# Gate and up products of two feed-forward blocks by a Strassen form: seven block products for eight, tokens in two halves

## The chip, the cores and the metric

The kernel runs on one core of a Trainium2 chip. The metric is the device time of one execution in microseconds (us); the runs shown of the kernel before have a median of 1450.88 us (three runs, 1450.59 to 1451.72).

## What is computed

A decoder trunk of two layers over 512 tokens of width 1024, in float32. Layer 0 mixes tokens with two kinds of attention, layer 1 with a Mamba-2 block; after each mixer stands a SwiGLU feed-forward block with a hidden width of 2816, on a normalized input. Cut to what matters here:

```python
def rmsnorm(x, w, eps=NORM_EPS):
    y = xf * lax.rsqrt(jnp.mean(xf * xf, axis=-1, keepdims=True) + eps)
    return (y * w.astype(jnp.float32)).astype(x.dtype)

def swiglu(h, w_gate, w_up, w_down):
    return (jax.nn.silu(h @ w_gate) * (h @ w_up)) @ w_down

h = h + swiglu(rmsnorm(h, ffn_norm[layer]), ffn_w_gate[layer], ffn_w_up[layer], ffn_w_down[layer])
```

## The kernel before, in words

**Layout.** Activations are held transposed: 8 chunks of 128 features (partitions) by 512 tokens. A weight tile of 128 input features by 128 output features is the stationary operand of a matmul, 512 tokens are the moving one, and the result is 128 output features by 512 tokens in one PSUM bank.

**Two-part operands.** For precision each operand is split in two float32r parts, high and low: ScalarE casts the tile to its high part, VectorE subtracts that from the tile to get the low part. A product is three matmuls, high by high, high by low, low by high (`proj`, L340 to L342). The inputs of a feed-forward block are `xh`, `xl`; the weights are `whi`, `wlo`.

**The weight stream.** `Stream` (L83) walks a list of weight loads of 128 x 1024 floats, 512 KB each: SyncE loads them into `wraw` (3 buffers, L104), ScalarE casts to `whi` (L117) and VectorE subtracts to `wlo` (L118), 3 buffers of each. `next` (L124) has the split of the load two places ahead issued before the matmuls of the present one. One load serves two chunks of one group of four output tiles, 24 matmuls.

**The feed-forward block** (`ffn`, L745). Gate and up come in 11 groups `t` of four output tiles (two of gate, then two of up). Each group has four loads, 8 chunks k, and 96 matmuls into four PSUM banks of the pool `acc`, which has four. Its evacuation `evac_gu` makes silu of a gate tile (ScalarE, L763), multiplies it by the up tile (VectorE, L767) and splits the product to `hh`, `hl` (L771, L772) for the down projection. The reciprocal root of the norm, `rbc`, is only known some time after the block starts: groups 0 and 1 run on inputs that have the norm's weight alone, and their results are multiplied by `rbc` when they are evacuated (L759). During group 1 the chunks are normalized and split anew, one by one (`normalized`, L354), and groups 2 to 10 read those. The down projection then takes 22 hidden tiles through `proj` (L340 to L342 again, tile `hh`); in layer 1 its last output tile is done by `finish` in two halves of 256 tokens (L1145 to L1147).

**What sets the order.** Work that lies beside the matmuls is a generator in `bg`; `proj` calls `bg.step(steps)` after each chunk k. The instructions are traced in program order. A planner then writes each engine's queue ahead of the run: among the instructions whose inputs it reckons ready when the engine comes free, the one that was traced first goes next. The engine takes its queue in that fixed order.

Of the kernel before, what the change touches and what calls it, by code (L numbers as in the profile page):

```python
# [25 lines left out]
LAMBDA_INIT = 0.8 - 0.6 * math.exp(-0.3 * 0)  # L26
KK = 2
LOOK = 2


SSD_ORDER = [
# [51 lines left out]
class Stream:  # L83


    def __init__(self, nc, pool, plan):
        self.nc, self.pool, self.plan = nc, pool, plan
        self.loaded = 0
        self.split = 0
        self.raw = {}  # L90
        self.parts = {}
        self.pos = 0
# [2 lines left out]
    def cuts(i, w):  # L95
        return ((0, w // 2), (w // 2, w)) if i == 0 else ((0, w),)

    def load_to(self, n):
        while self.loaded < min(n, len(self.plan)):
            ap, w = self.plan[self.loaded]  # L100
            i = self.loaded
            raw = self.pool.tile([P, 1024], F32, tag="wraw", name=f"wraw{i}", bufs=3)
# [3 lines left out]
            self.loaded += 1  # L106

    def split_to(self, n):
        while self.split < min(n, len(self.plan)):
            i = self.split  # L110
            self.load_to(i + 1)
            _, w = self.plan[i]
            raw = self.raw.pop(i)
            hi = self.pool.tile([P, 1024], F32R, tag="whi", name=f"whi{i}", bufs=LOOK + 1)
            lo = self.pool.tile([P, 1024], F32R, tag="wlo", name=f"wlo{i}", bufs=LOOK + 1)
            for c0, c1 in self.cuts(i, w):
                self.nc.scalar.copy(hi[:, c0:c1], raw[:, c0:c1])  # L117
                self.nc.vector.tensor_tensor(out=lo[:, c0:c1], in0=raw[:, c0:c1], in1=hi[:, c0:c1].bitcast(F32),  # L118
                                             op=ALU.subtract)
            self.parts[i] = (hi, lo)  # L120
            self.split += 1
            self.load_to(i + 3)

    def next(self):  # L124
        self.split_to(self.pos + LOOK + 1)
        r = self.parts.pop(self.pos)
        self.pos += 1
        return r


class Work:
# [21 lines left out]
def build(nc, tc, a):  # L153
    ctx = ExitStack()
    with ctx:
# [10 lines left out]
        def uid(s):  # L166
            count[0] += 1
            return f"{s}_{count[0]}"
# [16 lines left out]
        for t in range(2):  # L185
            plan += [(a["w_aout"][t * 4 + p], 1024) for p in range(4)]

        def ffn_plan(l):
            r = []
            for t in range(11):  # L190
                r += [(a[f"w_gu{l}"][t * 4 + p], 1024) for p in range(4)]
            for t, n in enumerate(DOWN_TILES[l]):
                r += [(a[f"w_down{l}_{t}"][i], KK * n * P) for i in range(11)]
            return r

        plan += ffn_plan(0)
# [33 lines left out]
        for n, (c0, c1) in enumerate(((0, 1), (1, 3), (3, 5), (5, 8))):  # L230
            nc.sync.dma_start(htile[0][:, c0:c1, :], xv[:, c0:c1, :])
            if n < 3:
                ws.load_to(n + 1)
# [82 lines left out]
        def proj(nk, ncols, get_x, evac, token_major=False, kk=KK, steps=0, width=2, wait=0):  # L316

            nt = 4 if token_major else (ncols + P - 1) // P
            ps = [None] * nt
            for p in range(nk // kk):  # L320
                whi, wlo = ws.next()
                for q in range(kk):
                    k = p * kk + q
# [26 lines left out]
        def x0get(k):  # L350
            done_k[0] = k
            return xh[k], xl[k]

        def normalized(norm):  # L354

# [389 lines left out]
        def ffn(l, norm, nxt, after, finish=None):  # L745
            with ExitStack() as fctx:
                fp = fctx.enter_context(tc.tile_pool(name=uid("ffn"), bufs=1))
                bg.add(norm.stats())
                hid = []

                gate = {}

                def evac_gu(t, j, ps):

                    if t < 2:
                        if t == 0:
                            bg.drain()
                        v = fp.tile([P, S], F32, tag="sg", name=uid("sg"), bufs=4)
                        tt(out=v, in0=ps, in1=norm.rbc, op=ALU.mult)  # L759
                        ps = v  # L760
                    if j < 2:
                        sg = fp.tile([P, S], F32, tag="sg", name=uid("sg"), bufs=4)
                        act(sg, ps, AF.Silu)  # L763
                        gate[j] = sg
                    else:
                        sg = gate.pop(j - 2)
                        tt(out=sg, in0=sg, in1=ps, op=ALU.mult)  # L767
                        n = len(hid)
                        hh = fp.tile([P, S], F32R, tag=f"hh{n}", name=uid("hh"))
                        hl = fp.tile([P, S], F32R, tag=f"hl{n}", name=uid("hl"))  # L770
                        nc.scalar.copy(hh, sg)  # L771
                        tt(out=hl, in0=sg, in1=hh.bitcast(F32), op=ALU.subtract)  # L772
                        hid.append((hh, hl))

                for t in range(11):
# [4 lines left out]
                    if t == 1:  # L780
                        for _ in xn:
                            pass
                        bg.drain()

                c0 = 0
                for n in DOWN_TILES[l]:
                    def evac_down(j, ps, c0=c0):
                        c = c0 + j
                        tt(out=h[c], in0=h[c], in1=ps, op=ALU.add)  # L789
                        nxt.chunk(c)  # L790
                        after(c)
                    proj(22, n * P, lambda k: hid[k], evac_down)
                    c0 += n
                if finish:
                    finish(hid)
# [365 lines left out]
def pack(w, groups, korder, kk):  # L1161

    r = []
    for cols in groups:
        m = np.concatenate([w[:, c0:c0 + n] for c0, n in cols], axis=1)
        for i in range(0, len(korder), kk):
            r.append(np.concatenate([m[k * P:(k + 1) * P] for k in korder[i:i + kk]], axis=1))
    return np.ascontiguousarray(np.stack(r))


def host_layout(x, attn_norm, attn_w_in, diff_lq1, diff_lk1, diff_lq2, diff_lk2, diff_subln, attn_w_out,
# [8 lines left out]
    d["w_aout"] = pack(attn_w_out[0], half, AO_K, KK)  # L1180
    for l in range(2):
        gu = np.concatenate([ffn_w_gate[l], ffn_w_up[l]], axis=1)
        d[f"w_gu{l}"] = pack(gu, [[(t * 256, 256), (DFF + t * 256, 256)] for t in range(11)], k8, KK)
# [54 lines left out]
```

## Time and profile before

| | |
|---|---|
| median of 3 runs | 1450.88 us |
| profiled execution, its own time | 1449.53 us |
| its span, first to last instruction | 1447.7 us |
| TensorE matmuls | 6755, busy 98% of the span |
| VectorE, ScalarE | busy 55% and 47% of the span |
| mean granted TensorE clock | 0.997 |

PE is TensorE's matmuls, PEld its weight loads, DVE VectorE, ACT ScalarE, POOL GpSimd, SP SyncE. A matmul's row shows its duration in the pipeline; the pace is the distance between two starts. The same holds for DVE and ACT, whose rows can overlap a little with the next.

### The profile page before, as it was taken

The numbers are of one execution on the slowest core, as the hardware profiler recorded it, in microseconds if no ns is written. First come the engines' busy times: TensorE is split into PE (matmuls) and PEld (weight loads), VectorE is DVE, ScalarE is ACT, GpSimd is POOL, SyncE is SP. The second block draws the span as 40 slices with busy tenths as digits, with TensorE's granted clock in tenths as the row PEclk, the third lists the DMA queues.
The fourth block names the chain that finished last, engine by engine and source line by source line (L and its number), as shares of the span: only waits on it lengthen the run. The fifth ranks groups of instructions, "written<-read, shape, count | busy, mean of one in ns | idle before, by whom it ended". The sixth has DMA issues, their size and how long they took to land.

```text
span 1447.7 us, 17120 instructions
## 1 busy us (share of the span) xinstructions
PE 1421.1 (98%) x6755; PEld 1168.3 (81%) x6755; DVE 797.7 (55%) x1145; ACT 681.8 (47%) x1137; POOL 21.5 (1%) x23
## 2 busy tenths in 40 slices
PE   9999899999999999999999999999999999999997
PEld 6777678888888888877888888887888888888886
DVE  7677995572333323247787684886556333333233
ACT  6555774342232222236879767594444233232131
POOL 0000001000000000000000000000000000000000
PEclk9999999999999999999999999999999999999998
DMA  6213241223233232333323223223232333333231
GB/s 217 88 35 97 65 126 59 88 87 116 89 102 98 92 102 88 128 111 105 129 101 102 102 88 119 100 73 130 88 102 87 102 91 99 103 89 100 84 106 59
DMA packets 41712, 142.83 MB, mean 99 GB/s; under 512 B 4736, under 2 KB 6912, under 8 KB 40224
## 3 DMA queue, kind: packets, MB, share of 16 engines
q1 hardware_dynamic: 40512, 140.68, 30.6%
q8 instruction: 53, 0.87, 0.2%
q10 hardware_dynamic: 1088, 1.05, 0.2%
q14 instruction: 27, 0.22, 0.0%
q0 software_dynamic: 32, 0.00, 0.0%
HBM read 135.36 MB, written 4.26 MB: 96 GB/s over the span
## 4 chain that ended last, share of the span: by engine, by line
PE 89%; DVE 5%; ACT 3%; issue 1%; POOL 1%; DMA 0%; SPq 0%; POOLq 0%; DVEq 0%; ACTq 0%
PE acc L340 24%; PE acc L342 24%; PE acc L341 24%; PE acc L333 2%; PE acc L335 2%; PE acc L334 2%; PE misc L1003 2%; DVE e L528 2%; PE misc L978 1%; PE misc L1008 1%; DVE wlo L118 1%; PE misc L496 1%; PE misc L948 1%; DVE e L530 0%; PE misc L1030 0%
## 5 line engine op out<-in xcount | busy, mean ns | idle before, releaser
L118 DVE TENSOR_TENSOR wlo<-wraw,whi 128x1024 fp32r<-128x1024 f32 (+3 forms) x230 | 276.2, 1202 | 446.9 <-ACT whi L117 444.8
L117 ACT CAST whi<-wraw 128x1024 fp32r<-128x1024 f32 (+3 forms) x230 | 238.0, 1035 | 486.7 <-PE acc L341 415.8
L340 PE MATMUL acc<-xnh,whi 128*128 128x512 f32 x808 | 319.7, 396 | 0.0
L341 PE MATMUL acc<-xnl,whi 128*128 128x512 f32 x808 | 316.9, 392 | 0.0
L342 PE MATMUL acc<-xnh,wlo 128*128 128x512 f32 x808 | 314.5, 390 | 0.0
L342 PEld LDWEIGHTS acc<-xnh,wlo 128*128 128x128 f32 x808 | 151.7, 188 | 31.9
L340 PEld LDWEIGHTS acc<-xnh,whi 128*128 128x128 f32 x808 | 151.7, 188 | 31.3 <-DVE sg L759 0.3
L341 PEld LDWEIGHTS acc<-xnl,whi 128*128 128x128 f32 x808 | 151.8, 188 | 30.1
L340 PE MATMUL acc<-hh,whi 128*128 128x512 f32 x330 | 128.5, 389 | 0.0
L342 PE MATMUL acc<-hh,wlo 128*128 128x512 f32 x330 | 128.4, 389 | 0.0
L341 PE MATMUL acc<-hl,whi 128*128 128x512 f32 x330 | 128.4, 389 | 0.0
L340 PE MATMUL acc<-xh,whi 128*128 128x512 f32 (+1 forms) x288 | 114.4, 397 | 1.9 <-DVE vl L467 1.1
L342 PE MATMUL acc<-xh,wlo 128*128 128x512 f32 (+1 forms) x288 | 113.2, 394 | 1.2 <-DVE wlo L118 1.2
L341 PE MATMUL acc<-xl,whi 128*128 128x512 f32 (+1 forms) x288 | 113.4, 394 | 0.2 <-DVE xl L279 0.2
L341 PEld LDWEIGHTS acc<-hl,whi 128*128 128x128 f32 x330 | 61.9, 188 | 12.9
L340 PEld LDWEIGHTS acc<-hh,whi 128*128 128x128 f32 x330 | 61.9, 188 | 12.9 <-DVE h L789 0.2
L342 PEld LDWEIGHTS acc<-hh,wlo 128*128 128x128 f32 x330 | 61.9, 188 | 12.9
L340 PEld LDWEIGHTS acc<-xh,whi 128*128 128x128 f32 (+1 forms) x288 | 53.5, 186 | 14.7 <-DVE vl L467 1.3
L342 PEld LDWEIGHTS acc<-xh,wlo 128*128 128x128 f32 (+1 forms) x288 | 53.5, 186 | 13.7 <-DVE wlo L118 2.1
L341 PEld LDWEIGHTS acc<-xl,whi 128*128 128x128 f32 (+1 forms) x288 | 53.6, 186 | 11.5 <-DVE xl L279 0.6
L767 DVE TENSOR_TENSOR sg<-sg,acc 128x512 f32<-128x512 f32 x36 | 24.5, 688 | 49.7 <-PE acc L342 41.2
L340 PE MATMUL acc<-ysh,whi 128*128 128x512 f32 x128 | 50.6, 395 | 0.0
(269 smaller groups left out, 2141.5 us busy)
## 6 DMA issues: line engine op xcount, KB each, us to landing
wraw<-w_gu SPq DMA_DIRECT2D x88, 512.0 KB, 3.6
wraw<-w_down SPq DMA_DIRECT2D x33, 512.0 KB, 3.6
wraw<-w_st SPq DMA_DIRECT2D x28, 512.0 KB, 3.5
wraw<-w_ain SPq DMA_DIRECT2D x23, 512.0 KB, 3.7
wraw<-w_sz SPq DMA_DIRECT2D x16, 512.0 KB, 3.2
h<-acd SPq DMA_DIRECT2D x8, 1024.0 KB, 4.8
wraw<-w_sout SPq DMA_DIRECT2D x16, 512.0 KB, 3.3
wraw<-w_down SPq DMA_DIRECT2D x11, 384.0 KB, 3.1
```

The lines of the kernel that those rows point to most:

```text
L117: self.nc.scalar.copy(hi[:, c0:c1], raw[:, c0:c1])
L118: self.nc.vector.tensor_tensor(out=lo[:, c0:c1], in0=raw[:, c0:c1], in1=hi[:, c0:c1].bitcast(F32), op=ALU.subtract)
L333: mm(o, ah[:, bs], whi[:, wc], start=first, stop=False)
L334: mm(o, ah[:, bs], wlo[:, wc], start=False, stop=False)
L335: mm(o, al[:, bs], whi[:, wc], start=False, stop=last)
L340: mm(o, whi[:, c0:c0 + m], ah, start=first, stop=False)
L341: mm(o, whi[:, c0:c0 + m], al, start=False, stop=False)
L342: mm(o, wlo[:, c0:c0 + m], ah, start=False, stop=last)
L496: nc.tensor.transpose(ps[:, n * P:(n + 1) * P], src[:, SEG[i] + j * P:SEG[i] + (j + 1) * P], ident)
L528: nc.vector.tensor_tensor_scan(out=keep[:, ::-1], data0=keep[:, ::-1], data1=endc[:, ::-1], initial=1.0, op0=ALU.mult, op1=ALU.max)
L767: tt(out=sg, in0=sg, in1=ps, op=ALU.mult)
L1003: mm(py[:, r * 64:(r + 1) * 64], bc[:, r, cs], xdt[:, c, r * 64:(r + 1) * 64], start=True, stop=True)
```

## The change

Groups 0 and 1 of gate and up stay as they are (`CONV = 2`). The other 18 output tiles of gate and their 18 of up are done in pairs: tile i of gate and tile i of up, tokens in halves, the eight input chunks in even (first) and odd (second) ones. The product of the 2 x 2 block weights with the 2 x 2 block inputs is made of seven block products instead of eight, named 11, 12, s2, s1, s3, 22 and s4. A block product is 4 chunks x 3 matmuls of 256 tokens. It needs sums of weight blocks and of input blocks:

- The input sums (`combos`) are made once per feed-forward block while groups 0 and 1 run, with `steps=2`; they replace `normalized`. In a first part each of four chunk pairs has two normalized products, four half-width differences and the splits for 11, s2 and 22. In a second part, as the old `xh`, `xl` chunks come free, the splits for 12, s4, s1 and s3.
- The weight sums: for s1 and s3 the DMA adds while it writes (a SyncE load, then a GpSimd-issued DMA with `accum_op=add`); for s2 and s4 VectorE adds two blocks before the split.
- Loads are per pair one of 512 KB (`w_g`, kept in `wraw` until s4 is split) and five of 256 KB, two of these accumulating. The loads run one step earlier than before in the rest of the kernel too.
- After the blocks, ScalarE and VectorE copy and add partial results between two PSUM banks (`o1`, `o3`) and SBUF. Hidden tiles of the pairs are kept unsplit and are split in the down projection (`hget`), up to three ahead. The last two blocks of the last pair run after the first load of the down projection.

The diff, cut to its core:

```diff
+CONV = 2
+NPAIR = NFF - 2 * CONV
 class Stream:
...
             hi = self.pool.tile([P, 1024], F32R, tag="whi", name=f"whi{i}", bufs=LOOK + 1)
...
+            if isinstance(ap, list):
+                work = [(slice(n * 512, n * 512 + 512), b[0].block(b[1], b[2]), b) for n, b in enumerate(ap)]
...
+            for cs, src, b in work:
+                src = src() if b else src
+                self.nc.scalar.copy(hi[:, cs], src)
+                self.nc.vector.tensor_tensor(out=lo[:, cs], in0=src, in1=hi[:, cs].bitcast(F32), op=ALU.subtract)
+                if b and b[0].done(b[1], b[2]):
+                    self.load()
...
-            self.load_to(i + 3)
+            if not isinstance(ap, list):
+                self.load()
+class Pairs:
...
+        for i in range(n + 1):
+            r += [(i, "11"), (i, "12")] if i < n else []
+            if i == n:
+                break
+            r += [(i - 1, "22"), (i - 1, "s4")] if i else []
+            r += [(i, "s2"), (i, "s1"), (i, "s3")]
+        self.order = r
+    def load(self, i, raw):
+        self.first[i] = raw
+        self.nc.sync.dma_start(raw, self.w11[i])
+        if i < 2:
+            for what in ("s1", "s3", "22"):
+                self.load_side(i, what)
+    def load_side(self, i, what):
...
+        if what == "s1":
+            self.nc.sync.dma_start(t, w21)
+            self.nc.gpsimd.dma_start(t, w22, accum_op=ALU.add)
+        elif what == "s3":
+            self.nc.sync.dma_start(t, self.w11[i, :, 0:512])
+            self.nc.gpsimd.dma_start(t, w21, accum_op=ALU.add)
+        else:
+            self.nc.sync.dma_start(t, w22)
+    def block(self, i, what):
...
+            if what == "s2":
+                self.nc.vector.tensor_tensor(out=a, in0=self.side[i, "s1"], in1=a, op=ALU.add)
+            elif what == "s4":
+                self.nc.vector.tensor_tensor(out=b, in0=a, in1=b, op=ALU.add)
...
+    def done(self, i, what):
+        if what in ("s1", "s3", "22"):
+            del self.side[i, what]
+            self.load_side(i + 2, what)
+        elif what == "s4":
+            del self.first[i]
+            return True
+        return False
+        def combos(norm, fp, xs):
...
+            def split(dst, src, cs=slice(0, S)):
+                hi, lo = dst
+                nc.scalar.copy(hi[:, cs], src)
+                tt(out=lo[:, cs], in0=src, in1=hi[:, cs].bitcast(F32), op=ALU.subtract)
...
+            for c in range(NCH // 2):
...
+                for o, n in ((xa, 2 * c), (xb, 2 * c + 1)):
+                    stt(out=o, in0=h[n], scalar=vcol(norm.w, n), in1=norm.rbc, op0=ALU.mult, op1=ALU.mult)
+                yield
+                tt(out=ta[:, H[0]], in0=xa[:, H[0]], in1=xa[:, H[1]], op=ALU.subtract)
+                tt(out=ta[:, H[1]], in0=xb[:, H[1]], in1=xa[:, H[1]], op=ALU.subtract)
+                stt(out=tb[:, H[0]], in0=ta[:, H[0]], scalar=-1.0, in1=xb[:, H[1]], op0=ALU.mult, op1=ALU.subtract)
+                stt(out=tb[:, H[1]], in0=tb[:, H[0]], scalar=-1.0, in1=xb[:, H[0]], op0=ALU.mult, op1=ALU.subtract)
+                yield
...
+                split(half[0], xa[:, H[0]], H[c % 2])
...
+                split(e, tb)
...
+                yield
+            for c in range(NCH // 2):
+                while done_k[0] < 2 * c + 1:
+                    yield
...
+                e = xpair(2 * c, "xc")
+                split(e, xb)
...
+                e = xpair(2 * c + 1, "xc")
+                split(e, ta)
...
+                yield
-                for t in range(11):
-                    if t == 1:
-                        xn = normalized(norm)
-                        bg.add(xn)
-                    proj(8, 512, x0get if t == 1 else xget, lambda j, ps: evac_gu(t, j, ps), steps=1 if t < 2 else 0)
...
+                for t in range(CONV):
+                    proj(8, 512, x0get if t == CONV - 1 else xget, lambda j, ps: evac_gu(t, j, ps), steps=2)
...
+                def block(i, what, whi, wlo):
+                    if what == "11":
+                        o1[i] = bank("misc")
+                    elif what == "12":
+                        o2[i] = bank("acc")
+                    elif what == "s1":
+                        o3[i] = bank("misc")
+                    o = {"12": o2, "s1": o3, "s4": o3}.get(what, o1)[i][:, A]
...
+                    for c in range(NCH // 2):
+                        wc = slice(c * P, (c + 1) * P)
+                        ah, al = xs[what, c]
+                        mm(o, whi[:, wc], ah, start=new and c == 0, stop=False, skip_group_check=True)
+                        mm(o, whi[:, wc], al, start=False, stop=False, skip_group_check=True)
+                        mm(o, wlo[:, wc], ah, start=False, stop=end and c == NCH // 2 - 1, skip_group_check=True)
...
+                    if what == "11":
+                        sg[i] = fp.tile([P, S], F32, tag="gate", name=uid("sg"), bufs=2)
+                        nc.scalar.copy(sg[i][:, A], o1[i][:, A])
+                    elif what == "12":
+                        tt(out=sg[i][:, A], in0=sg[i][:, A], in1=o2[i][:, A], op=ALU.add)
+                    elif what == "s2":
+                        nc.scalar.copy(sg[i][:, B], o1[i][:, A])
+                    elif what == "s3":
...
+                        nc.scalar.copy(hl[:, B], o1[i][:, A])
+                        tt(out=hl[:, B], in0=hl[:, B], in1=o3[i][:, A], op=ALU.add)
+                    elif what == "s4":
...
+                        tt(out=sg[i][:, B], in0=sg[i][:, B], in1=o3[i][:, A], op=ALU.add)
+                        act(sg[i], sg[i], AF.Silu)
+                        stt(out=hl[:, A], in0=o1[i][:, A], scalar=-1.0, in1=sg[i][:, A], op0=ALU.mult, op1=ALU.mult)
+                        stt(out=hl[:, B], in0=hl[:, B], scalar=-1.0, in1=sg[i][:, B], op0=ALU.mult, op1=ALU.mult)
...
+                blocks(pr.order)
...
+                def hget(k):
+                    for n in range(k, min(k + 3, len(hid))):
+                        split_hid(n)
+                    return hid[k]
```

## Rows read from the trace of the kernel before

**Rows 1.** Page, part 1: busy time, share of the span, instructions.
```profile
PE 1421.1 (98%) x6755; PEld 1168.3 (81%) x6755; DVE 797.7 (55%) x1145; ACT 681.8 (47%) x1137; POOL 21.5 (1%) x23
```

**Rows 2.** Chain that ended last: share of the span by engine.
```profile
PE 89%; DVE 5%; ACT 3%; issue 1%; POOL 1%; DMA 0%; SPq 0%; POOLq 0%; DVEq 0%; ACTq 0%
```

**Rows 3.** Windows: stretch; PE, PEld, DVE, ACT, POOL busy; clock; DMA share; GB/s.
```profile
336.50:553.00 216.50, 216.50 (x957) 179.27 (x956) 71.85 (x76) 61.52 (x76) 0.00 (x0) 1.00 0.32 98
1310.00:1425.00 115.00, 115.00 (x529) 96.06 (x528) 37.77 (x44) 33.47 (x45) 0.00 (x0) 1.00 0.27 83
1439.50:1440.00 0.50, 0.00 (x0) 0.00 (x0) 0.00 (x0) 0.00 (x0) 0.50 (x1) 0.76 0.00 0
1440.00:1440.50 0.50, 0.38 (x2) 0.38 (x3) 0.00 (x0) 0.00 (x0) 0.06 (x1) 0.50 0.00 0
```

**Rows 4.** Timeline of PE in block zero's gate and up, 18 starts apart.
```profile
399.70 0.39 PE L340 MATMUL acc<-xnh,whi 128*128 128x512 f32 x1
...
403.78 0.39 PE L340 MATMUL acc<-xnh,whi 128*128 128x512 f32 x1
```

**Rows 5.** Timeline of PE, last projection, 22 starts apart; then its weight loads.
```profile
1434.01 0.28 PE L1146 MATMUL acc<-hl,wlh 128*128 128x256 f32 x1
...
1436.65 0.28 PE L1147 MATMUL acc<-hh,wll 128*128 128x256 f32 x1
...
L1145 PEld LDWEIGHTS acc<-hh,wlh x44: 188/192/192, 1419.8 to 1436.3; 128*128 128x128 f32 x44
```

**Rows 6.** Timeline of DVE: instructions that follow at once on each other.
```profile
824.78 0.68 DVE L993 TENSOR_TENSOR h<-h,cb 128x512 f32<-128x512 f32 x1
825.38 0.74 DVE L908 SCALAR_TENSOR_TENSOR fb<-u,vec,fb 128x510 f32<-128x510 f32 x1
...
834.61 1.22 DVE L970 TENSOR_TENSOR xdt<-xs,dtt 128x1024 f32<-128x1024 f32 x1
835.74 1.22 DVE L118 TENSOR_TENSOR wlo<-wraw,whi 128x1024 fp32r<-128x1024 f32 x1
...
837.21 0.42 DVE L991 TENSOR_TENSOR xs<-xs,vec 128x256 f32<-128x256 f32 x1
837.55 0.41 DVE L986 TENSOR_TENSOR prev<-prev,misc 128x256 f32<-128x256 f32 x1
```

**Rows 7.** Groups by line and form, DVE and ACT: busy, mean ns.
```profile
L772 DVE TENSOR_TENSOR hl<-sg,hh 128x512 fp32r<-128x512 f32 x44 | 28.4, 685 | 0.6 <-ACT hh L771 0.6
L771 ACT CAST hh<-sg 128x512 fp32r<-128x512 f32 x44 | 25.4, 618 | 2.6 <-DVE sg L767 2.6
L763 ACT ACTIVATE sg<-sg 128x512 f32<-128x512 f32 x8 | 5.0, 631 | 8.2 <-DVE sg L759 8.1
```

**Rows 8.** Timeline near the end: DVE hands over to ACT.
```profile
1428.17 0.42 DVE L1115 TENSOR_TENSOR h<-h,acc 128x256 f32<-128x256 f32 x1 [4.64 <-PE acc L1147]
...
1428.62 0.42 ACT L1116 ACTIVATE up<-h 128x256 f32<-128x256 f32 x1 [5.06 <-DVE h L1115]
```

**Rows 9.** Timeline of DVE at the start of block zero's feed-forward.
```profile
271.31 2.05 DVE L739 TENSOR_TENSOR h<-h,acc 128x512 f32<-128x512 f32 x3 [1.32 <-PE acc L342]
273.27 0.75 DVE L279 SCALAR_TENSOR_TENSOR xl<-h,vec,xh 128x512 fp32r<-128x512 f32 x1
...
277.07 0.68 DVE L739 TENSOR_TENSOR h<-h,acc 128x512 f32<-128x512 f32 x1
...
284.60 1.41 DVE L361 SCALAR_TENSOR_TENSOR xn<-h,vec,rbc 128x512 f32<-128x512 f32 x2 [2.96 <-ACT rbc L314]
...
295.15 2.80 DVE L759 TENSOR_TENSOR sg<-acc,rbc 128x512 f32<-128x512 f32 x4 [1.32 <-PE acc L342]
```

**Rows 10.** Timeline of PE: warm-up matmuls at the start.
```profile
2.29 4.01 PE L239 MATMUL misc<-warm 128*128 128x512 bf16 x9 [2.29 <-ACT warm L236]
```

**Rows 11.** Queues and DMA issues: packets, MB, share; KB, us to landing.
```profile
q1 hardware_dynamic: 40512, 140.68, 30.6%
vec<-vec POOLq DMA_DIRECT2D x1, 4.0 KB, 3.1
```

More of the change, by code (lines that the diff above doesn't have):

```diff
@@ L87, in __init__ @@
         self.nc, self.pool, self.plan = nc, pool, plan
+        self.loads = []
+        for i, (ap, w) in enumerate(plan):
+            if isinstance(ap, list):
+                self.loads += [(b[0], b[1]) for b in ap if b[2] == "11"]
+            else:
+                self.loads.append((None, i))
         self.loaded = 0
@@ L96, in cuts, with load @@
         return ((0, w // 2), (w // 2, w)) if i == 0 else ((0, w),)
[L98 to L102, printed above, removed]
+    def load(self, n=1):
+        for _ in range(n):
+            if self.loaded == len(self.loads):
+                return
+            owner, i = self.loads[self.loaded]
+            raw = self.pool.tile([P, 1024], F32, tag="wraw", name=f"wraw{self.loaded}", bufs=3)
+            self.loaded += 1
+            if owner:
+                owner.load(i, raw)
+                continue
+            ap, w = self.plan[i]
             for c0, c1 in self.cuts(i, w):
@@ L128, in next, with __init__, items, last @@
         return r
+class Pairs:
+    def __init__(self, nc, w11, w2, n):
+        self.nc, self.w11, self.w2, self.n = nc, w11, w2, n
+        self.tile = None
+        self.first = {}
+        self.side = {}
+        r = []
+        for i in range(n + 1):
[5 more added lines that the diff above has]
+        self.order = r
+    def items(self):
+        b = [(self, i, what) for i, what in self.order]
+        return [(b[i:i + 2], 1024) for i in range(0, len(b), 2)]
+    def last(self):
+        return [([(self, self.n - 1, "22"), (self, self.n - 1, "s4")], 1024)]
+    def load(self, i, raw):
[5 more added lines that the diff above has]
+    def load_side(self, i, what):
+        if i >= self.n:
+            return
+        t = self.side[i, what] = self.tile({"s1": 0, "s3": 2, "22": 4}[what] + i % 2)
+        w21, w22 = self.w2[i, 0], self.w2[i, 1]
+        if what == "s1":
[4 more added lines that the diff above has]
+            self.nc.gpsimd.dma_start(t, w21, accum_op=ALU.add)
+        else:
+            self.nc.sync.dma_start(t, w22)
+    def block(self, i, what):
+        def get():
+            first = self.first[i]
+            a, b = first[:, 0:512], first[:, 512:1024]
+            if what == "s2":
+                self.nc.vector.tensor_tensor(out=a, in0=self.side[i, "s1"], in1=a, op=ALU.add)
+            elif what == "s4":
+                self.nc.vector.tensor_tensor(out=b, in0=a, in1=b, op=ALU.add)
+            return {"11": a, "s2": a, "12": b, "s4": b}.get(what) if what not in ("s1", "s3", "22") \
+                else self.side[i, what]
+        return get
+    def done(self, i, what):
[6 more added lines that the diff above has]
+        return False
 class Work:
@@ L314, in stats, with proj @@
                 nc.scalar.copy(self.rbc, pb)
-        def proj(nk, ncols, get_x, evac, token_major=False, kk=KK, steps=0, width=2, wait=0):
+        def proj(nk, ncols, get_x, evac, token_major=False, kk=KK, steps=0, width=2, wait=0, hook=None):
             nt = 4 if token_major else (ncols + P - 1) // P
@@ L747, in ffn, with after_stats @@
                 fp = fctx.enter_context(tc.tile_pool(name=uid("ffn"), bufs=1))
+                pr = pairs[l]
+                pr.tile = lambda n: fp.tile([P, S], F32, tag=f"hh{4 + n}", name=uid("ws"))
+                done_k[0] = -1
+                xs = {}
                 bg.add(norm.stats())
+                def after_stats():
+                    while norm.rbc is None:
+                        yield
+                    yield from combos(norm, fp, xs)
+                xc = after_stats()
+                bg.add(xc)
@@ L773, in evac_gu @@
[L773 to L783 removed]
+                        tt(out=v, in0=gate.pop(j - 2), in1=v, op=ALU.mult)
@@ new lines, in blocks, with tail @@
+                def blocks(order):
+                    for m in range(0, len(order), 2):
+                        whi, wlo = ws.next()
+                        for q, (i, what) in enumerate(order[m:m + 2]):
+                            cs = slice(q * 512, q * 512 + 512)
+                            block(i, what, whi[:, cs], wlo[:, cs])
+                blocks(pr.order)
+                def tail(p):
+                    if p == 1:
+                        blocks([(NPAIR - 1, "22"), (NPAIR - 1, "s4")])
```

97 lines of the change are left out of this document (70 added, 27 removed).

## Prediction, made before the changed kernel ran

> **What bounds the kernel now.** I read the page first: TensorE's matmuls are busy 98% of the span, VectorE (DVE) 55%, ScalarE (ACT) 47% [rows 1]; but a share says little where stages differ, so I went on to the chain that ended last, 89% of which is PE [rows 2]. Then the windows of the stretch that the change touches: in block zero's feed-forward PE has no idle time, DVE works 71.85 of 216.5 us, ACT 61.52, and the DMA engines are a third busy [rows 3]. So the pace of the matmuls sets the time. The timeline of PE gives that pace: 4.08 us for 18 starts, 0.2267 us for one matmul of 512 columns [rows 4]. The same kernel already has matmuls of 256 columns with a weight load each, in its last projection: 2.64 us for 22 starts, 0.120 us each, though one weight load lasts 0.19 us [rows 5]: the loads lie under the matmuls. Half the columns cost a little more than half the time.
>
> **The matmuls.** A pair of output tiles now takes 2 x 8 x 3 = 48 matmuls of 512 columns, 48 x 0.2267 = 10.88 us. The seven blocks take 7 x 4 x 3 = 84 of 256 columns, 84 x 0.120 = 10.08 us. So 0.80 us of the 1.36 us that an eighth would be is kept; 36 pairs in two blocks give **-28.8 us**. That is the whole gain.
>
> **What the other engines must do in 10.08 us.** Of DVE I need the distance from one instruction to the next where none waits: 0.60 us for 512 elements, 0.34 for 256, 1.13 for 1024, each 0.08 shorter than its duration [rows 6]. Per pair DVE has seven subtractions for the low parts (7 x 0.605 = 4.24), two additions for s2 and s4, and evacuations of 256 columns: an addition each for 12, s3 and s4, and two products. In three places it cannot run on, unless other work is ready: behind the s2 and the s4 addition stands a cast by ACT (0.618) and behind the s4 evacuation a silu (0.631) [rows 7], each with two hand-overs of 0.03 [rows 8]. So an addition with its cast takes 0.685 + 0.618 + 0.06 = 1.36, twice 2.73; the evacuations 2 x 0.335, then 0.42 + 0.631 + 0.06 = 1.11, then 2 x 0.335: 2.45. Sum 9.41 us, under PE's 10.08. With full durations in place of distances it is 7 x 0.685 + 2.73 + 2 x 0.42 + 1.11 + 2 x 0.42 = 10.31, 0.23 over, which is 36 x 0.23 = 8 us. The bounds are 0 and +8 us; the busy stretch of rows 6 runs at distances, so I stay near the lower end: **+3 us**. ACT has seven casts, three copies and a silu, under 7 x 0.62 + 3 x 0.42 + 0.63 = 6.2 us: hidden.
>
> One wait is tight on PE: s3 accumulates in the bank that ACT must first have copied after s2, and only s1 (12 x 0.12 = 1.44 us) lies between. A cast just begun and the copy take about 0.62 + 0.42 = 1.04: it fits, so nothing; if ACT hangs behind DVE, PE waits there (rival two).
>
> **Transfers.** A pair moves 512 + 5 x 256 KB, 1.84 MB, against 1 MB. The present queue carries 140.68 MB in 30.6% of 1447.7 us, 318 GB/s at full share [rows 11]. The plain part, 1.31 MB, needs 4.1 us of 10.08. No row shows an accumulating DMA. As a plain copy its 0.26 MB would take 0.8 us of all engines; the one GpSimd-issued DMA here needs 3.1 us from issue to landing, 4 KB only [rows 11]; if two such stood in series with the rest, 4.1 + 6.2 = 10.3 us would just pass the pair's time. They are asked for two pairs (20 us) ahead, so latency is hidden and only throughput counts; I take 0, as nearer to the copy. The Trainium skill's page "DMA: Bandwidth & Descriptors" (Anatomy of one DMA) prices a GpSimd-issued DMA at about 2.0 us plus its bytes at 436 GB/s, by estimate 2.6 us for 256 KB and nothing on the sum; it says nothing of accumulation. SyncE issues two loads more per pair, GpSimd two; both queues hold little else in this stage, and each waits for buffers freed two pairs before their next use: nothing.
>
> **The seam between groups 0 and 1.** Here I expect the gain to be given back. The planner's order shows in DVE's queue: the fourth addition to `h` goes at 277.07, behind work on the earlier chunks though its matmuls had long ended [rows 9]. What was traced first goes first, once ready. Now `steps=2` traces all twelve steps of the first part of `combos` before the evacuation of group 0. They need `rbc`, first used at 284.60 [rows 9]; until then they can't start. Per chunk pair: two products of 0.66 (1.41 for two with overlap [rows 9]), four half-width operations of 0.335, a half split of 0.335 and one of 0.605: 1.32 + 1.34 + 0.34 + 0.61 = 3.6, four times 14.4. Two weight splits of 1.13 stand between: 16.7. So DVE is at this until 284.6 + 16.7 = 301.3. The last split waits for its cast, so the first evacuation slips in at 300.7 and ends at 301.4. Before, it began at 295.15, and four took 2.80 us, at PE's pace [rows 9]; so PE is done with group 0 at about 297.2. Group 1 needs the four `acc` banks that group 0 holds, and no weights of later work are split yet. PE stands 301.4 + 0.1 - 297.2 = 4.3 us. The bounds are 0, if the evacuation goes first, and 7, if all four evacuations (2.8 us) must end first. I take 4.3, which is what the banks ask for. At the end of the trace the granted clock fell from 1.00 to 0.50 (2.4 to 1.2 GHz) between 1439.5 and 1440.0 [rows 3]; PE had done little since the last projection ended at 1436.65 [rows 5]. So I expect it to fall in this pause too. At the start nine warm-up matmuls of 512 columns took 4.01 us [rows 10], 0.446 each against 0.2267: coming back costs 9 x 0.22 = 2.0 us (bounds 0 and 2; I take 2). Together 6.3 per block, twice **+12.6 us**.
>
> **The seam before the pairs.** When group 1 ends, DVE owes eight operations of evacuation, two late splits and one item's two: 12 x 0.605 = 7.3 us, of which 1.9 lie before that end. PE can go on with 11, 12, s2 and s1, 4 x 1.44 = 5.8 us: even. If 12 has to wait for its last chunk, after 1.44 + 1.08, it costs 5.4 - 2.5 = 2.9. I take 0.5, twice **+1 us**.
>
> **Costed at nothing.** The down projection now splits 18 hidden tiles per block itself: a cast and 0.605 us of DVE per 12 x 0.2267 = 2.72 us of PE; there DVE works 37.77 of 115 us [rows 3]. Without that cover it would be 18 x 1.3 per block. Loads one step earlier: PE waits for none of them.
>
> **The sum**, against the profiled execution's own 1449.5: 1449.5 - 28.8 + 3 + 12.6 + 1 = 1437.3. That execution is 1.4 us below the median, 1450.9; on the runs' scale **1439 us**.
>
> **Rivals.**
> *One: the seam is no wait.* The planner places the evacuations first, or finds other matmuls. For it: in nearly the whole trace it keeps PE busy [rows 1]; against it: rows 9. Then only the 28.8 counts: 1422, with some waits 1425. Chance 0.21.
> *Two, the other side: DVE and ACT set the pair's pace.* If ACT reaches each of its two late casts only behind an operation of 256 columns (0.42 [rows 8]), DVE's chain at full durations is 10.31 + 0.84 = 11.15 us. PE then stands before s3, and the price is (11.15 - 10.08) x 36 = 38 us, 35 more than the 3 taken: 1474. It decides at 10.08 + (28.8 - 13.6) / 36 = 10.5 us per pair: above that the change loses. For it: 9.41 of 10.08 is little slack; against: a planner can fill two of the three waits. Chance 0.20.
> *Three: the accumulating DMAs are slow.* At 4 us of all engines each, five times a copy, a pair takes 4.1 + 8 = 12.1 us: +2.0 x 36 = 73 us, 1509. For it: nothing shown. Chance 0.10.
> *Four: weight loads don't hide.* In series a block's matmul would take 0.12 + 0.19 = 0.31, the pair 26 us, 36 x 15.9 = +570: 2010. Rows 5 speak against it: starts 0.120 apart. The Trainium skill's "TensorE: Matmul & The Clock Gate" (The mechanism) has a load overlap a running matmul only when its row group differs; by that rule this rival would hold, and the trace disagrees. Chance 0.01.
>
> **How the numbers follow.** My forecast has 0.48; its own range is 1430 to 1450 (seams at their bounds, 0 to 8 us in the pairs). About 0.2% is what a measurement here can tell from no change: 1448.0 to 1453.8. Faster: 0.41 of the forecast and all of rival one, 0.62. Same: 0.07 of the forecast and 0.05 of rival two, 0.12. Slower: the rest of two, three, four: 0.26. The range takes in rival one and the lower part of rival two, up to 10.8 us per pair: 1422 to 1463.
>
> **What would show it.** Right: 256-column starts 0.120 us apart in both blocks; a pause of some 4 us before group 1 with DVE on `combos`, released by the L759 evacuation, and 0.50 clock after it. Wrong: no such pause (rival one); PE waiting for ACT's copy in each pair (two); ACT or DVE waiting for the side tiles' DMA, DMA share near 1 (three); starts over 0.2 us apart (four).

## The result: 1436.1 us, 1.0% faster

The changed kernel takes 1436.1 us (median of four, 1434.9 to 1437.3); the kernel before, beside it on the same chip, 1450.7. The ratio is 0.990, 95% interval 0.988 to 0.992. The prediction said 1439, 1422 to 1463. The profiled execution took 1434.85 us with a span of 1432.7, against 1449.53 and 1447.7 before: 15.0 us of span went.

### The profile page after: what moved, and what is told of

Its sections match the earlier page's. It is cut to its first block, busy times and chain, and to the rows that moved or that the text cites. A ratio compares the mean times of both kernels' runs of the same rounds, so it can differ in the third digit from the quotient of the medians.

```text
span 1432.7 us, 20958 instructions
## 1 busy us (share of the span) xinstructions
PE 1396.3 (97%) x8051; PEld 1208.7 (84%) x8051; DVE 974.9 (68%) x1589; ACT 789.5 (55%) x1441; POOL 83.6 (6%) x95
## 3 DMA queue, kind: packets, MB, share of 16 engines
q1 hardware_dynamic: 50880, 150.13, 31.2%
q0 software_dynamic: 10400, 18.88, 8.4%
## 4 chain that ended last, share of the span: by engine, by line
PE 85%; DVE 9%; ACT 3%; issue 2%; DMA 1%; POOL 1%; SPq 0%; DVEq 0%; POOLq 0%; ACTq 0%
PE acc L439 15%; PE acc L440 14%; PE acc L441 14%; PE misc L965 7%; PE misc L966 7%; PE misc L967 7%; PE acc L432 2%; PE acc L434 2%; PE acc L433 2%; PE misc L1224 2%; DVE e L679 2%; PE acc L967 1%; PE acc L965 1%; PE acc L966 1%; DVE wlo L136 1%
## 5 line engine op out<-in xcount | busy, mean ns | idle before, releaser
L136 DVE TENSOR_TENSOR wlo<-wraw,whi 128x512 fp32r<-128x512 f32 (+3 forms) x302 | 284.6, 952 | 264.5 <-ACT whi L135 262.5
L135 ACT CAST whi<-wraw 128x512 fp32r<-128x512 f32 (+3 forms) x302 | 248.2, 833 | 331.9 <-PE acc L440 228.0
L965 PE MATMUL misc<-xe,whi 128*128 128x256 f32 x432 | 122.4, 283 | 0.0
L966 PE MATMUL misc<-xcl,whi 128*128 128x256 f32 x432 | 122.3, 283 | 0.0
L967 PE MATMUL misc<-xch,wlo 128*128 128x256 f32 x432 | 122.3, 283 | 0.0
L966 PE MATMUL misc<-xe,whi 128*128 128x256 f32 x432 | 122.2, 283 | 0.0
L965 PE MATMUL misc<-xch,whi 128*128 128x256 f32 x432 | 122.2, 283 | 0.0
L439 PE MATMUL acc<-xnh,whi 128*128 128x512 f32 x232 | 95.7, 412 | 0.0
L440 PE MATMUL acc<-xnl,whi 128*128 128x512 f32 x232 | 92.8, 400 | 0.0
L441 PE MATMUL acc<-xnh,wlo 128*128 128x512 f32 x232 | 90.7, 392 | 0.0
L965 PEld LDWEIGHTS misc<-xe,whi 128*128 128x128 f32 x432 | 82.9, 192 | 0.4
L966 PEld LDWEIGHTS misc<-xe,whi 128*128 128x128 f32 x432 | 82.9, 192 | 0.2
```

Source lines behind the costliest of these rows:

```text
L135: self.nc.scalar.copy(hi[:, cs], src)
L136: self.nc.vector.tensor_tensor(out=lo[:, cs], in0=src, in1=hi[:, cs].bitcast(F32), op=ALU.subtract)
L439: mm(o, whi[:, c0:c0 + m], ah, start=first, stop=False)
L440: mm(o, whi[:, c0:c0 + m], al, start=False, stop=False)
L441: mm(o, wlo[:, c0:c0 + m], ah, start=False, stop=last)
L965: mm(o, whi[:, wc], ah, start=new and c == 0, stop=False, skip_group_check=True)
```

## The profile after

The page of the changed kernel first (busy time, then two queues, then three groups of DMA issues with KB and median us to landing):

```profile
PE 1396.3 (97%) x8051; PEld 1208.7 (84%) x8051; DVE 974.9 (68%) x1589; ACT 789.5 (55%) x1441; POOL 83.6 (6%) x95
...
q1 hardware_dynamic: 50880, 150.13, 31.2%
q0 software_dynamic: 10400, 18.88, 8.4%
...
ws<-w_u SPq DMA_DIRECT2D x72, 256.0 KB, 3.9
ws<-w_u POOLq DMA_DIRECT2D x72, 256.0 KB, 5.0
wraw<-w_g SPq DMA_DIRECT2D x36, 512.0 KB, 4.7
```

PE has 1296 instructions more than in [rows 1] and is busy 24.8 us less; DVE has taken on 177 us, ACT 108. The queue q0 is new: the accumulating DMAs. But the page doesn't say where the time went. PE's landmarks do: the first matmul of a feed-forward block, the first 256-column matmul, the last one.

**The pairs.** The timeline of PE, around the first pair of block zero and then in its middle (start, duration, engine and line, operation):

```profile
326.51 0.39 PE L441 MATMUL acc<-xh,wlo 128*128 128x512 f32 x1
326.73 0.28 PE L965 MATMUL misc<-xe,whi 128*128 128x256 f32 x1
...
400.33 0.28 PE L965 MATMUL misc<-xe,whi 128*128 128x256 f32 x1
400.45 0.28 PE L966 MATMUL misc<-xe,whi 128*128 128x256 f32 x1
```

The windows inside the pairs of both blocks (columns as in [rows 3]):

```profile
330.00:500.00 170.00, 170.00 (x1418) 170.00 (x1418) 130.33 (x241) 96.33 (x194) 26.56 (x31) 1.00 0.69 175
1120.00:1295.00 175.00, 175.00 (x1459) 174.88 (x1459) 135.28 (x248) 99.98 (x200) 27.04 (x32) 1.00 0.67 171
```

The pairs begin 0.22 us after the last matmul of group 1, so there is no pause; starts are 0.120 us apart, as in the old last projection [rows 5]; PE is busy without a gap, at a clock of 1.00, in both blocks. The last start before the down projection is at 505.33: 178.60 us for 1488 steps, and the last two blocks (24 starts, 2.9 us) follow in the down projection. That makes 181.5 us per block where groups 2 to 10, 864 matmuls at 0.2267 [rows 4], took 195.9: **28.8 us less in two blocks**, to the tenth what the matmuls alone were to give. DVE is busy 77% of the stretch.

**The seam.** PE's longest wait over the whole span (tile and line, what ended it; us in total, times, longest):

```profile
PE acc L439 <- DVE sg L931: 8.8, 2, 4.4
```

PE's timeline around the start of group 1 in block zero, and its first start in block one (in brackets the idle time before, and what ended it):

```profile
298.32 0.39 PE L441 MATMUL acc<-xh,wlo 128*128 128x512 f32 x1
303.10 0.47 PE L439 MATMUL acc<-xh,whi 128*128 128x512 f32 x1 [4.39 <-DVE sg L931]
...
303.63 0.60 PE L441 MATMUL acc<-xh,wlo 128*128 128x512 f32 x1
304.21 0.79 PE L439 MATMUL acc<-xh,whi 128*128 128x512 f32 x1
304.80 0.63 PE L440 MATMUL acc<-xl,whi 128*128 128x512 f32 x1
305.23 0.63 PE L441 MATMUL acc<-xh,wlo 128*128 128x512 f32 x1
...
306.93 0.46 PE L439 MATMUL acc<-xh,whi 128*128 128x512 f32 x1
...
1096.16 0.77 PE L439 MATMUL acc<-xh,whi 128*128 128x512 f32 x1 [4.39 <-DVE sg L931]
```

DVE's timeline at the same time:

```profile
301.59 0.43 DVE L479 SCALAR_TENSOR_TENSOR tb<-tb,xb 128x256 f32<-128x256 f32 x1
301.92 0.43 DVE L463 TENSOR_TENSOR xe<-xa,xe 128x256 fp32r<-128x256 f32 x1
302.26 0.69 DVE L931 TENSOR_TENSOR sg<-acc,rbc 128x512 f32<-128x512 f32 x1
302.86 0.69 DVE L463 TENSOR_TENSOR xe<-tb,xe 128x512 fp32r<-128x512 f32 x1
303.46 1.89 DVE L931 TENSOR_TENSOR sg<-acc,rbc 128x512 f32<-128x512 f32 x3
```

The window around it:

```profile
298.00:309.00 11.00, 6.61 (x22) 4.62 (x21) 11.00 (x20) 6.52 (x10) 0.00 (x0) 0.84 0.26 77
```

DVE has no idle time between 298 and 309; it works on `combos` (L463 to L479) and one weight split, and the first evacuation of group 0 (L931) begins only at 302.26, with one split of their first part left behind it. PE stands 4.39 us, in each block. Then the granted clock of the window is 0.84: the nine starts from 303.10 to 306.93 take 3.83 us against 9 x 0.2267 = 2.04, 1.8 more; in block one six starts take 2.69 against 1.36, 1.3 more. The stretch from block zero's first feed-forward matmul to the first matmul behind group 1 is 45.61 us before (273.14 to 318.75) and 52.05 after (274.68 to 326.73): 6.4 us given back.

**Before the block** the changed kernel is 1.5 us late: 274.68 for 273.14. The prediction had put that at nothing.

## The experiments

### e1_steps: the evacuation ahead of most combos

```diff
-proj(8, 512, x0get if t == CONV - 1 else xget, lambda j, ps: evac_gu(t, j, ps), steps=2)
+proj(8, 512, x0get if t == CONV - 1 else xget, lambda j, ps: evac_gu(t, j, ps), steps=1 if t == 0 else 2)
```

> The edit traces one step of the combos instead of two between the steps of group 0, so the first evacuation of group 0 is traced ahead of most of them. Theory (the planner gives DVE the work that was traced first, so the combos hold up the evacuation, and PE waits 4.39 us for it and then runs 1.3 to 1.8 us longer on a halved clock): the pause before group 1 is gone in both blocks, 2 x (4.4 + 1.5) = 11.8 us less, the profile near 1423 us (1422 to 1427, as up to 4 us may come back where the pairs start, since the combos end later). Rival (the evacuation is late for another reason, such as rbc itself or the banks): the pause stays at 4.4 us in each block and the time near 1435.

Measured: 1422.2 us (1421.7 to 1422.4), 0.980 of the kernel before (0.979 to 0.982), and span 1419.5. DVE's timeline now:

```profile
294.53 0.70 DVE L463 TENSOR_TENSOR xe<-tb,xe 128x512 fp32r<-128x512 f32 x1
295.13 0.76 DVE L474 SCALAR_TENSOR_TENSOR xb<-h,vec,rbc 128x512 f32<-128x512 f32 x1
295.79 2.49 DVE L931 TENSOR_TENSOR sg<-acc,rbc 128x512 f32<-128x512 f32 x4
298.18 0.43 DVE L476 TENSOR_TENSOR ta<-xa 128x256 f32<-128x256 f32 x1
```

All four evacuations go at 295.79, between two steps of `combos`; the wait is gone in both blocks. From the first feed-forward matmul to the first pair it is 45.59 us (273.50 to 319.09), the 45.61 of the kernel before; from block zero's first pair to block one's 786.58 instead of 792.62. So the seam cost 6.46 + 6.04 = **12.5 us**, and it is an order of tracing, not work: DVE does the same operations. Nothing comes back at the pairs' start: PE has no wait there, and the last split of `combos` starts 2.3 us behind the first pair in both kernels. The medians are 13.9 us apart; this trace came 1.2 us earlier to the block (273.50 for 274.68).

### e2_warm: the pause kept, TensorE kept busy

```diff
 proj(8, 512, x0get if t == CONV - 1 else xget, lambda j, ps: evac_gu(t, j, ps), steps=2)
+if t == 0:
+    pk = bank("misc")
+    for n in range(18):
+        mm(pk, warm[:, :P], warm, start=n == 0, stop=n == 17)
```

> The edit puts 18 matmuls on zeros, into a bank that nobody reads, between group 0 and the wait. Theory (the slow starts 0.43 us apart behind the pause are the clock, which falls because PE stands): the wait for the evacuation still ends at the same instant, but the clock stays at 1.00 and group 1 begins with starts 0.227 us apart, 1.8 + 1.3 = 3.1 us less, near 1431.7 us. Rival (these matmuls are slow because banks come free one by one): the same slow starts behind the extra matmuls, near 1434.9 us.

Measured: 1431.4 us (1430.9 to 1432.9). PE's timeline:

```profile
299.71 4.06 PE L946 MATMUL misc<-warm 128*128 128x512 bf16 x18
304.27 0.47 PE L439 MATMUL acc<-xh,whi 128*128 128x512 f32 x1 [0.50 <-DVE sg L931]
304.58 0.39 PE L440 MATMUL acc<-xl,whi 128*128 128x512 f32 x1
304.81 0.39 PE L441 MATMUL acc<-xh,wlo 128*128 128x512 f32 x1
```

Its window:

```profile
299.00:310.00 11.00, 10.50 (x47) 6.86 (x46) 11.00 (x20) 6.80 (x11) 0.00 (x0) 1.00 0.23 78
```

The evacuation still ends the wait at the same distance from the block's start (28.41 us for 28.42), but the clock stays at 1.00 and the starts come 0.23 apart. Between the landmarks of e1_steps it saves 1.79 and 1.39 us, 3.2 against 3.1 expected. The medians differ by 4.7 us, the profiled executions by 2.0, because this one came 1.2 us later to its feed-forward (275.86 for 274.68), which is ahead of the edit.

### e3_dve3 and e4_dve6: more work for DVE in each pair

```diff
 n = 2 * CONV + i
+if what in ('11', 's1', '22'):
+    dum = trunk.tile([P, S], F32, tag="sq", name=uid("dum"), bufs=2)
+    tt(out=dum, in0=norm.rbc, in1=norm.rbc, op=ALU.mult)
```

(e4_dve6 does it for '11', '12', 's2', 's1', 's3' and '22'.)

> The edit adds three multiplications of 128 x 512 on DVE to each pair, 3 x 0.605 = 1.8 us. Theory A (DVE's pair is a chain in order of 9.41 us, with the waits for ACT's casts in it): 9.41 + 1.8 = 11.2 us against PE's 10.08, 36 x 1.1 = 41 us more, near 1476 us. Theory B (other work fills DVE's waits for ACT, so only the sum of the distances counts, some 7.13 us a pair): 8.9 us, still under 10.08, 0 to 3 us more.

> The edit adds six such multiplications to each pair, 6 x 0.605 = 3.63 us. Theory B (waits filled): 7.13 + 3.63 = 10.76 us, 0.68 over PE's 10.08, 36 x 0.68 = 24 us more, near 1459 us, with DVE busy without a gap in the pairs. Theory A (chain in order): 13.0 us, 36 x 2.9 = 106 us more, near 1541 us.

Measured, one run each: 1437.8 and 1449.8 us. The window from the first pair's first start to the last start before the down projection, in e3_dve3:

```profile
327.60:506.22 178.62, 178.62 (x1489) 178.49 (x1487) 160.74 (x297) 103.00 (x206) 27.42 (x32) 1.00 0.66 170
```

The same stretch in e4_dve6, and then for its added line alone:

```profile
329.65:513.79 184.14, 182.56 (x1489) 179.40 (x1487) 182.35 (x338) 101.32 (x202) 27.48 (x32) 1.00 0.65 162
```

```profile
329.65:513.79 184.14, 61.73 (x92) 1.00 0.65 162
```

Three more operations cost the pairs nothing: 178.62 us for 178.60. Six make the stage 5.5 us longer, in block one as well (1128.20 to 1312.35), and DVE is busy 99% of it. Theory A falls: a chain in order would have shown +41 already with three. DVE's waits for ACT's casts are filled with other work. DVE's wait for the cast between 330 and 500, in the changed kernel and then in e4_dve6:

```profile
DVE wlo L136 <- ACT whi L135: 29.0, 33, 1.7
```

```profile
DVE wlo L136 <- ACT whi L135: 0.5, 1, 0.5
```

The wait shrinks as there is more to do, so it was slack. Theory B expected +24 and got 11 in the pairs: only 92 of block zero's 108 multiplications fell into the stage (the row of L971 alone), 13 were done before it and 3 behind it. With these 92 its sum comes out: 18 x 7.13 + 92 x 0.605 = 184.0 us, for 184.14 measured. A pair needs DVE for some 7.1 us, and can give it up to 10.

### e5_late and e7_both: the loads one step later

```diff
 if not isinstance(ap, list):
-    self.load()
+    self.load(0 if i == 0 else 2 if i == 31 else 1)
```

> The edit asks for each weight tile up to the feed-forward one step later, as the kernel before does. Theory (the loads one step earlier move a transfer in front of one that attention waits for): the wait of 1.09 us before the output projection is 0.31 again and the feed-forward of block 0 starts 0.8 to 1.5 us earlier, the median 1434.6 to 1435.3 us. Rival (the start is scatter between executions): 1436 us, the wait unchanged.

> The edit joins the one step of the combos of e1_steps and the later weight loads of e5_late. Theory (the gain of e1_steps, and the 0.8 us that the matmuls after the first projection of attention's output wait longer for a weight part, 1.09 for 0.31 us, are independent): e1_steps's 1422.2 less 0.8, near 1421.4 us. Rival (the longer wait is scatter of the first loads, as the start of the kernel already differs by 2 us between executions): 1422.2 us.

Measured: e5_late 1435.4 us (1434.2 to 1438.2), e7_both 1421.9 (1420.9 to 1423.9). PE's wait before the output projection of attention, in the kernel before, the changed kernel and e5_late:

```profile
189.51 0.50 PE L334 MATMUL acc<-wlo,xh 128*128 128x512 f32 x1 [0.31 <-DVE wlo L118]
```

```profile
191.09 0.50 PE L433 MATMUL acc<-wlo,xh 128*128 128x512 f32 x1 [1.09 <-DVE wlo L136]
```

```profile
189.62 0.50 PE L433 MATMUL acc<-wlo,xh 128*128 128x512 f32 x1 [0.29 <-DVE wlo L136]
```

The wait is 0.29 us in e5_late and e7_both, as good as the 0.31 of before, and 1.08 to 1.10 in the traces of e1_steps, e2_warm, e3_dve3 and e4_dve6, which load early as the changed kernel does. So 0.8 us of the 1.5 is the change's own and comes with the earlier loads. How is not shown: in the changed kernel ACT had cast that weight tile by 184.75, and DVE's subtraction started only at 189.81, behind other work of attention with hardly a gap from 181 on; so it was not the tile's own load that came late, but DVE's queue that was in another order. The medians can't tell it: in the traces of the changed kernel, e1_steps, e2_warm, e3_dve3 and e4_dve6, whose code is the same up to there, the last wait of attention (L761) ends between 239.73 and 243.95. The other 0.7 us are within that scatter. e7_both is no different from e1_steps; those two are the best versions here, 14 us under the changed kernel.

### e6_acc2, e9_free and e10_order: twice the accumulating DMAs

In e6_acc2 each is issued twice on the same tile; in e9_free and e10_order it has a twin on one of three tiles that nobody reads (the third, `hl4`, lies where a hidden tile's low part goes later). The edit of e10_order, for s1 (s3 has the same; `mark` copies two columns of `t` to the next of the three tiles on GpSimd and returns that tile):

```diff
 self.nc.sync.dma_start(t, w21)
+d = self.mark(t)
 self.nc.gpsimd.dma_start(t, w22, accum_op=ALU.add)
+self.nc.gpsimd.dma_start(d, w22, accum_op=ALU.add)
```

> The edit issues each accumulating DMA twice, so that the sums s1 and s3 of the weights hold their second addend twice. Theory (only the share of the DMA engines counts): a pair's two more DMAs take 2 x 1.67 = 3.3 us of all engines, the share in the pairs goes from 0.67 to 1.0 and a pair needs about 10.1 to 10.3 us, 0 to 10 us more in all (up to 1446 us). Rival (accumulating DMAs run one behind the other at their 5.0 us from issue to landing): 20 us a pair against 10.08, 357 us more, near 1790 us.

> The edit gives each accumulating DMA a twin of 256 KB that adds the same weights to one of three tiles that nobody reads, so that no transfer waits for the one before it on its own tile, as in e6_acc2. Theory (in e6_acc2 the pairs were held up by the chain: a second addition waits until the first on the same tile has landed, and with it GpSimd's queue): without the chain only the share counts, 0.67 + 0.33 = 1.0 of the DMA engines, 0 to 10 us more than the changed kernel's profile, at most 1445 us. Rival (two more accumulating DMAs a pair overload the DMA engines themselves): about the time of e6_acc2, 1514 us.

> As e9_free, but each twin goes out beside its own pair: GpSimd copies two columns of the side tile, when its plain load has landed, into the twin's tile, so that the twin cannot be issued sooner (in e9_free the planner sent all 36 of a block at the block's start). Theory (without a chain on one tile only the share of the DMA engines counts): the pairs run at a share of 0.67 + 2 x 1.62 / 10.08 = 0.99, 10.1 to 10.4 us a pair, 0 to 12 us more than the changed kernel's profile. Rival (accumulating DMAs delay one another or GpSimd's queue beyond their share): over 10.5 us a pair, PE waits for side tiles as in e6_acc2, 15 to 80 us more.

Measured, one run each: 1513.6, 1472.2 and 1453.6 us. In **e6_acc2** neither theory holds: +77, not 10 and not 357. GpSimd's waits there between 340 and 510:

```profile
POOL ws L192 <- DMA ws<-w_u: 44.5, 14, 5.4
```

L192 is the second addition; 14 times it waits for the first to land, and what stands behind it in GpSimd's queue waits too. In the same stretch DVE's addition for s2 waits 35.8 us for the side tile. So it tested a chain, and e9_free was to take the chain away. That run is **inconclusive** for its question: nothing tied a twin to its own pair, the planner sent all 36 of a block at its start, and the small operation that leads to `rbc` stood behind them in the same queue. PE's longest wait in e9_free:

```profile
PE misc L411 <- POOL rtok L407: 32.8, 2, 17.3
```

The queues of e9_free between 300 and 345, where almost only twins ran:

```profile
q0 software_dynamic: 3409, 6.23, 85.3%
q1 hardware_dynamic: 597, 2.14, 13.6%
```

6.23 MB in 85.3% of 45 us are 162 GB/s at full share. **e10_order** puts each twin beside its own pair. Its windows:

```profile
340.00:500.00 160.00, 154.85 (x1290) 154.49 (x1288) 115.35 (x216) 85.15 (x171) 62.35 (x90) 0.99 0.95 224
1130.00:1300.00 170.00, 166.47 (x1382) 165.74 (x1380) 122.74 (x229) 90.05 (x181) 63.98 (x95) 1.00 0.97 222
```

The DMA engines are 95 to 97% busy. The stage takes 186.49 us (327.27 to 513.76) and 187.92 (1128.60 to 1316.52) instead of 178.6, 17 us more in all, but most of that is not the transfers' doing. PE's idle time in the first window, 160.00 less 154.85, is a single wait:

```profile
494.57 0.28 PE L981 MATMUL misc<-xch,wlo 128*128 128x256 f32 x1
500.00 0.58 PE L979 MATMUL misc<-xch,whi 128*128 128x256 f32 x1 [5.15 <-ACT sg L989]
```

Behind it stands DVE's longest wait in that window, for a twin:

```profile
DVE hl L936 <- DMA du<-w_u: 7.3, 1, 7.3
```

DVE's split of a hidden tile, done ahead for the down projection, writes the buffer of the twins' third tile and stands until the twin has landed; ACT's and PE's next work stands behind it, and the granted clock is 0.57 from 500 to 506. The same happens in block one (5.13 us before 1303.23). That is a side effect of the shared buffer, not a price of the transfers. Up to that wait each block makes 1392 starts, in 167.29 and 169.22 us for the changed kernel's 167.08: 0.2 and 2.1 us more, 10.1 and 10.2 us a pair. The run as a whole, 17 us more, falls into the rival's range, but the pairs keep to the theory: by this the share of the engines is what counts. The change's own accumulating DMAs leave a third of the engines' time free, and double their number nearly fills them and costs PE next to nothing. How the full run would come out without the shared buffer, no run shows.

### e8_cols: is it the columns?

```diff
-mm(o, whi[:, wc], al, start=False, stop=False, skip_group_check=True)
-mm(o, wlo[:, wc], ah, start=False, stop=end and c == NCH // 2 - 1, skip_group_check=True)
+mm(o[:, :P], whi[:, wc], al[:, :P], start=False, stop=False, skip_group_check=True)
+mm(o[:, :P], wlo[:, wc], ah[:, :P], start=False, stop=end and c == NCH // 2 - 1, skip_group_check=True)
```

> The edit lets two of the three matmuls of each product (those with a low part) run over 128 columns instead of 256, so the low parts are left out for half of the tokens of each half. Theory A (0.120 us is the pace of the weight load, 128 x 128 for each matmul, or another cost of each matmul that has nothing to do with columns): starts stay 0.120 apart and the time near 1435 us. Theory B (the pace goes with the columns, half of it per half): 0.120 + 2 x 0.06 for three, 6.7 us a pair, under DVE's 7.1, which then sets the pace: 36 x 2.9 = 105 us less, near 1330 us.

Measured, one run: 1435.8 us. The timeline of PE:

```profile
399.98 0.33 PE L965 MATMUL misc<-xch,whi 128*128 128x256 f32 x1
400.14 0.22 PE L966 MATMUL misc<-xcl,whi 128*128 128x128 f32 x1
400.20 0.28 PE L967 MATMUL misc<-xch,wlo 128*128 128x128 f32 x1
400.32 0.33 PE L965 MATMUL misc<-xch,whi 128*128 128x256 f32 x1
```

The window inside the pairs:

```profile
330.00:500.00 170.00, 166.77 (x1452) 165.34 (x1452) 134.50 (x248) 97.22 (x196) 26.74 (x31) 1.00 0.67 175
```

And PE's longest wait over the span:

```profile
PE misc L965 <- ACT sg L975: 9.2, 20, 2.6
```

Three matmuls with 512 columns in all take 0.34 us; with 768 columns they took 0.36. In 170 us PE makes 1452 starts for 1418, and 3.2 us of the 170 it waits. A third of the columns is worth 4 to 6% of the pace: at 256 columns a matmul already costs nearly what it costs whatever its columns. From 512 to 256 the columns still set the pace, 0.2267 to 0.120, so the floor lies just under 0.120. Theory A holds but for that; that this floor is the weight load's is likely, not shown apart. New waits eat part of that gain: L975 is ACT's copy after s2, and with s1 shorter PE now stands before s3, the place that the prediction called tight. The stage takes 176.54 us for 178.60 in block zero and 175.74 for 178.61 in block one. The one run's time shows none of these 4.9 us; it came with a mean granted clock of 0.988 for 0.995.

The Trainium skill's "TensorE: Matmul & The Clock Gate" (LDWEIGHTS) gives a formula for the load by its columns, by estimate 107 ns for 128, and its section Back-to-back issue gap says that load and matmul together set the spacing. The 0.113 us of these rows lies near that estimate, but a load's own row lasts 0.19 us [rows 5]. The 81 ns that the second section gives for 128 columns is shown by no run here.

## Why the prediction was right, and where its sizes were off

- **The matmuls, -28.8 us:** 28.8. The 0.120 us of the old last projection held for all 36 pairs.
- **What the other engines must do, +3 us:** measured 0. This is the step that was mis-sized. It put DVE's waits for ACT into the pair's time one after the other, 9.41 or 10.31 us; e3_dve3 and e4_dve6 show that the planner fills them, so that the sum of the distances counts, 7 x 0.605 + 2 x 0.605 + 5 x 0.335 = 7.1 us, which PE's 10.08 hide. The text had that argument, but only against rival two ("a planner can fill two of the three waits"), and rival two, at 0.20, had too much.
- **The bank between s2 and s3:** no wait of PE there in either block. It is as tight as it was called: in e8_cols, where s1 is a little shorter, PE waits there 20 times.
- **Transfers, 0:** right; PE never waited for them. The 72 accumulating DMAs take 8.4% of 1432.7 us of all engines, 1.67 us each, where a plain copy of 0.26 MB was put at 0.8; rival three needed 4. One takes 5.0 us from issue to landing, for the 2.6 of the prediction's estimate. By e10_order the limit lies near twice their number.
- **The seam between groups 0 and 1, +12.6 us:** 12.5 by e1_steps. The reason was right: what is traced first goes first. So was its length: `combos` start at 286.17, the first evacuation 16.1 us later at 302.26, as worked out (284.6 to 300.7), in a block that itself starts 1.5 us later. The wait is 4.39 us for 4.3, or 4.55 by the distance of the starts (298.32 to 303.10, less 0.2267), the clock 1.8 and 1.3 us for 2.0 each (e2_warm: 3.2 together). So the wait was put a little too low and the clock a little too high; that the sum meets to a tenth is luck.
- **The seam before the pairs, +1 us:** 0; the first pair follows at 0.22 us, though the last split of `combos` starts 2.3 us behind it.
- **Loads one step earlier, costed at nothing:** 0.8 us (e5_late). PE waited for none of the loads themselves, but for the split of a weight part that stood later in DVE's queue; why the queue's order changed with the loads is open.
- **The down projection's own splits:** no new wait; from its first start to its last it takes 122.49 us in block zero, 119.56 before, and the two blocks that moved into it are 2.9 of that.

Together, -28.8 + 12.5 + 0.8 = -15.5 us of span against -15.0 measured; with the other 0.7 us of the late start, which lie within the scatter, it is -14.8. The forecast of 1439 was 3 us high because two small charges, +3 and +1, weren't there and one of 0.8 was missing. Rival one's 1422 us, the gain without the seam, is what e1_steps measures.

## What to carry to other kernels

When background work is traced ahead of an evacuation that frees PSUM banks, price it as a wait of PE: add up that work from the moment its input is ready, and compare with the end of the matmuls; spreading it over two groups was one number in the code and worth as much as nearly half the algorithm's gain. Halving the columns of a matmul to save products pays down to 256 columns here and hardly below. For an engine that isn't the bound, add up distances, not the chain, as long as other work stands ready to fill its waits, as the neighbouring pair's does here. And where an experiment gives a dummy a buffer, see who takes that buffer next: in e10_order most of the time that seemed to be the transfers' price was a wait for it.

## What the runs showed of the hardware that was not expected

- A 128 x 128 by 256 matmul costs 0.120 us against 0.2267 for 512 columns, but still 0.113 on average when two of three have 128 columns only (e8_cols).
- Accumulating DMAs move 18.88 MB in 8.4% of the span, 157 GB/s at full share, and 162 GB/s where they run almost alone (e9_free); the plain queue moves 150.13 MB in 31.2%, 336 GB/s. So an accumulating DMA takes about twice the engines' time of a load of the same bytes. Whether that is the addition, GpSimd's queue or its packets (1.8 KB for 3.0 on average) no run tells apart. With the engines 95 to 97% busy PE kept its pace of 0.120 us (e10_order, block zero up to 494.57).
- After the same 4.39 us pause the starts slow down from the third of group 1 in block zero (303.63, the next 0.58 us later) and from the first in block one (1096.16); with matmuls on zeros in the pause the granted clock stayed at 1.00 (e2_warm).
